# One-pass broadcasts of stacked high and low parts, and row halves of the array in turn, in a two-block sequence model

## The chip, the cores and the metric

The kernel runs on one core of one Trainium2 chip. The metric is device time in microseconds (us); the number that counts is the median of several runs. The engines have their own in-order instruction queues: TensorE (PE; its weight loads stand apart as PEld), VectorE (DVE), ScalarE (ACT), GpSimd (POOL) and SyncE (SP), which issues most of the DMAs.

## The reference

It computes one layer of a first block and two layers of a second one on a sequence of 512 positions with 1024 features. In the first block attention over a band of chunks stands beside an S5 state-space mixer, then come memory attention and a table of 16384 experts, of which each position picks some. A layer of the second block has three branches, of which two use decays along the sequence (SSD and a gated delta rule, GDN), then a feed-forward part. What the change touches:

```python
def _rmsnorm(x, g):
    xf = x.astype(jnp.float32)
    y = xf * lax.rsqrt(jnp.mean(xf * xf, axis=-1, keepdims=True) + EPS)
    return (y * g.astype(jnp.float32)).astype(x.dtype)
...
    bu_r = jnp.einsum('blgc,gpc->blgp', uf, bbr)
    bu_i = jnp.einsum('blgc,gpc->blgp', uf, bbi)
...
    y = (jnp.einsum('blgp,gcp->blgc', xr, c_re.astype(jnp.float32))
         - jnp.einsum('blgp,gcp->blgc', xi, c_im.astype(jnp.float32))
         + d_skip.astype(jnp.float32) * uf)
...
    L = jnp.exp(jnp.where(tril, A_cum[..., :, None] - A_cum[..., None, :], -jnp.inf))
...
    decay = jnp.exp(jnp.where(incl, g[..., :, None] - g[..., None, :], -jnp.inf))
```

Norms need one number per position, and decays one number per position and head, for all features at once.

## The kernel before

Activations lie with features on the 128 partitions and positions along the free axis, 512 (`T`) at a time. Large products are made of three one-pass products (`mm3`, lines 162 to 164): a value is split into a high part `H` and a low part `L` (`split`: ScalarE rounds to `H`, line 140; VectorE subtracts, line 141), and high times high, high times low and low times high are summed in PSUM. Small products are left in fp32, which the array does in more than one pass; the trace has two records for each.

Work is written as Python generators that run in turn, and the tile framework sets the order in which each engine issues; TensorE then works through its list in that order. PSUM has five buffers named `s`, two `g` and one `o`.

Four places matter here.

- A number per position on one column, `r` (128 positions by 4 blocks), comes from `rsqrt` on VectorE (its last line is 134). `rowbc` (line 179) makes of it a row that stands on all 128 partitions: for each block of 128 positions it takes the column, repeated 128 times, as weights, and the identity as the moving operand (line 183), four fp32 products. It serves every norm: 38 calls on 512 columns, five on 256 (in `memory_kv`). In `pair` of `mixers` four transpositions (816), a copy (818) and two products with the selecting matrix `sel` of 4 rows (821) do the same for two heads at once, four times.
- `Layer.rows` (line 1435) puts the cumulated decay of head `j` on all partitions: the transposed decays are kept as `cumT`, a high and a low tensor of 24 rows, and two one-pass products of 24 rows (line 1440) with a column of a 24 by 24 identity sum them. It is called 16 times by `ssd` (two calls at once) and 8 times by `gdn_prep_pair` in each of the two layers, that is 48 times.
- `S5.matrices` makes, for each of four blocks of groups, the taps `kt` (lines 607, 608): 16 products of 64 rows with 16 output rows, first all of the lower 64 partitions (`gh` 0), then all of the upper. They go by a POOL DMA to `kd` and back as `toep`.
- `S5.run` makes the outputs of a block: for each of its eight groups one product with `toep` (128 rows, line 661) and two of 64 rows with `car` and `cai` (662, 663), one group after the other.

Of the kernel before, what the change touches and what calls it, by code (L numbers as in the profile page):

```python
# [11 lines left out]
F32 = mybir.dt.float32  # L12
F32R = mybir.dt.float32r
I32 = mybir.dt.int32
U32 = mybir.dt.uint32
AF = mybir.ActivationFunctionType
OP = mybir.AluOpType
# [4 lines left out]
P = 128  # L22
T = 512
# [3 lines left out]
def f32(ap):  # L27
    return ap.bitcast(F32)
# [21 lines left out]
class Builder:  # L50
# [65 lines left out]
        self.tri = tri  # L116


    def rsqrt(self, out, x, scale, eps):

        nc, shape = self.nc, list(x.shape)
        v = self.small(shape)
        nc.vector.tensor_scalar(v, x, float(scale), float(eps), op0=OP.mult, op1=OP.add)
        sh = self.small(shape, I32)
        nc.vector.tensor_scalar(sh, v.bitcast(I32), 1, None, op0=OP.logical_shift_right)
        y = self.small(shape)
        nc.vector.tensor_scalar(y.bitcast(I32), sh, -1, 0x5F3759DF, op0=OP.mult, op1=OP.add)
        for i in range(3):
            a = self.small(shape)
            nc.vector.tensor_tensor(a, y, y, op=OP.mult)  # L130
            b = self.small(shape)
            nc.vector.scalar_tensor_tensor(b, a, -0.5, v, op0=OP.mult, op1=OP.mult)
            y2 = out if i == 2 else self.small(shape)
            nc.vector.scalar_tensor_tensor(y2, b, 1.5, y, op0=OP.add, op1=OP.mult)
            y = y2
# [43 lines left out]

    def rowbc(self, ps, col, n=T):  # L180

        for tb in range(n // P):
            self.nc.tensor.matmul(ps[:, tb * P:(tb + 1) * P],  # L183
                                  col[:, tb:tb + 1].to_broadcast([P, P]), self.ident,
                                  start=True, stop=True)

    def sumsq(self, srcs, n=T, w2=None):
        nc = self.nc
# [298 lines left out]
class S5:  # L487
# [57 lines left out]
    def matrices(self, q):  # L545
# [5 lines left out]
        m = t([P, 4, 4, 16], "s5m", 1)  # L551
# [45 lines left out]
                                B.ident[:16, :16].unsqueeze(1).to_broadcast([16, 8, 16]), op=OP.mult)  # L597
        kd = B.t([16, 8, 15, 16], F32, "kd", 2, B.dr)

        for gh in range(2):  # L600
            kt = t([16, 4, 15, 16], "kt")
            nc.vector.memset(kt[:, :, 0:7], 0.0)
            lo = 64 * gh
            ps = B.pss()
            for g in range(4):
                o = ps[:16, g * P:(g + 1) * P]
                nc.tensor.matmul(o, bbr[lo:lo + 64, g], car[lo:lo + 64, g, 0:8], start=True, stop=False)
                nc.tensor.matmul(o, bbi[lo:lo + 64, g], cai[lo:lo + 64, g, 0:8], start=False, stop=True)
            nc.scalar.copy(kt[:, :, 7:15], ps[:16].rearrange("p (g k c) -> p g k c", g=4, k=8))
            yield  # L610
            nc.vector.tensor_tensor(kt[:, :, 7], kt[:, :, 7], dd[:, gh::2], op=OP.add)
            nc.gpsimd.dma_start(kd[:, gh::2], kt)
# [5 lines left out]
    def run(self, u, mats, outer):  # L618
# [34 lines left out]
            v.tensor_tensor(out[:, :, 1:64], x[:, :, 0:63], y[:, :, 0:63], op=op)  # L653
        yg = t([P, 8, 64], "yg", 1)
        yield
        for gh in range(2):
            lo = 64 * gh
            ps = B.pss()
            for g in range(4):
                o = ps[:, 64 * g:64 * g + 64]  # L660
                nc.tensor.matmul(o, toep[:, 2 * g + gh], U[:, 2 * g + gh], start=True, stop=False)
                nc.tensor.matmul(o, car[lo:lo + 64, g, 1:9], xr[lo:lo + 64, g], start=False, stop=False)
                nc.tensor.matmul(o, cai[lo:lo + 64, g, 1:9], xi[lo:lo + 64, g], start=False, stop=True)
            nc.scalar.activation(yg[:, gh::2], ps[:, :256].rearrange("p (g j) -> p g j", g=4), AF.Gelu)
        yd = B.t([8, 16, 8, 64], F32, "yd", 2, B.dr)
        for s in range(8):
            nc.sync.dma_start(yd[:, :, s].rearrange("g c j -> c g j"), yg[16 * s:16 * s + 16])
# [62 lines left out]
def mixers(B, vec, memory, new_h):  # L730
# [3 lines left out]
    with tc.tile_pool(name="mixers", bufs=1) as pool:  # L734
# [2 lines left out]
        nc.vector.memset(hm[0:64, 0:1], 1.0)  # L737
        nc.vector.memset(hm[64:128, 1:2], 1.0)

        sel = B.t([4, 2, P], F32, "sel", 1, pool)  # L740
        nc.vector.memset(sel, 1.0)
        for base, sign in ((0, 1), (63, -1)):
            nc.gpsimd.affine_select(out=sel, in_=sel, pattern=[[P * sign, 2], [sign, P]], compare_op=OP.is_ge,
                                    fill=0.0, base=base, channel_multiplier=-64 * sign)
        xq = [B.t([P, T], F32, "qk", 8, pool) for _ in range(8)]
        for k in range(8):
            nc.sync.dma_start(xq[k], B.d["xT"][k])
# [47 lines left out]
        def pair(j):  # L795
# [18 lines left out]
            rt = B.pss()  # L814
            for tb in range(4):
                nc.tensor.transpose(rt[:4, tb * P:(tb + 1) * P], r[:, 4 * tb:4 * tb + 4], B.ident)
            rT = B.w2()[:4]
            nc.scalar.copy(rT, rt[:4])
            for i in range(2):
                ps = B.pss()  # L820
                nc.tensor.matmul(ps, sel[:, i], rT, start=True, stop=True)
# [408 lines left out]
class Second:  # L1230
# [5 lines left out]
    def setup(self, pool):  # L1236
# [20 lines left out]
            aff(c3, c3, [[s, P // s], [0, s]], OP.is_gt, 0.0, s, -1)  # L1257
        v.tensor_tensor(self.cross, self.cross, self.blk, op=OP.subtract)
        v.tensor_tensor(self.cross, self.cross, self.low, op=OP.mult)
        self.eye = B.t([24, 24], F32R, "eye", 1, pool)  # L1260
        v.tensor_copy(self.eye, B.ident[:24, :24])
        yield

        self.rot = B.t([P, P], F32R, "rot", 1, pool)
# [22 lines left out]
class Layer:  # L1287
# [73 lines left out]
    def decays(self, xs, rs):  # L1361
# [57 lines left out]
        pt = B.pss()  # L1419
        for tb in range(4):  # L1420
            nc.tensor.transpose(pt[:24, tb * P:(tb + 1) * P], self.cum[:, tb], B.ident)
        self.cumT = [B.t([24, T], F32R, "cumT" + k, 1, pool) for k in "HL"]
        B.split(pt[:24], *self.cumT)

        self.etot, self.eleft = t([P, 4, 24], "etot"), t([P, 4, 24], "eleft")
        nc.scalar.activation(self.etot, tot, AF.Exp)
# [7 lines left out]
    def rows(self, j):  # L1434

        B = self.B
        ps = B.pss()
        one = self.S.eye[:, j:j + 1].to_broadcast([24, P])
        for k, x in enumerate(self.cumT):
            B.nc.tensor.matmul(ps, one, x, start=k == 0, stop=k == 1)  # L1440
        return ps


# [561 lines left out]
```

## Time and profile before

| what | value |
|---|---|
| median of 3 runs | 4712.33 us (4710.74 to 4717.49) |
| the profiled execution | 4713.34 us |
| its span, first to last instruction | 4711.3 us |
| PE busy | 4638.6 us (98%), 22296 instructions |
| DVE busy | 2838.5 us (60%) |
| ACT busy | 1905.1 us (40%) |
| chain that ended last | PE 88%, DVE 8%, DMA 1%, ACT 1% |
| mean granted TensorE clock | 0.987 |

A busy share says how long some instruction of the engine was under way. Records of products overlap, so what a product costs in a stream is the distance from its start to the start of the next. The chain is followed back from the last instruction, at each step to what released it. The granted clock is given as a share of 2.4 GHz; it is 1.0 or 0.5 at any moment.

### The profile page before, as it was taken

To read this page: it belongs to the slowest core of one execution; us is meant where nothing else is said; L and a number is where in the kernel's file an instruction comes from. 1 tells how busy PE (TensorE), PEld (TensorE's weight loads), DVE (VectorE), ACT (ScalarE), POOL (GpSimd) and SP (SyncE) were. 2 spreads that over 40 slices of the span, in tenths; PEclk is the share of its full clock that TensorE was granted. 3 is DMA by queue.
4 is the path that set the end of the run, shared out by engine and by line. 5 is a ranking of instruction groups with operands and counts; after the bars stand their busy time and mean duration, and the time that the engine had idled before them with its cause. 6 is when DMAs were issued, how large, how long until landed. Compare 5 with 4: busy or idle time off the path is not lost.

```text
span 4711.3 us, 59345 instructions
## 1 busy us (share of the span) xinstructions
PE 4638.6 (98%) x22296; PEld 3718.0 (79%) x22296; DVE 2838.5 (60%) x5744; ACT 1905.1 (40%) x3652; POOL 29.0 (1%) x59
## 2 busy tenths in 40 slices
PE   8989999999999999999999999999999999999998
PEld 6777788888888888887787678888877876888887
DVE  8655799665545555556776545544478765545434
ACT  3343458763222222323553433333355535333322
POOL 0000000000000000000000000000000000000000
PEclk9789999999999999999999999999999999999999
DMA  4232235564434443442254155423324532544332
GB/s 133 68 97 76 83 124 182 201 205 152 132 123 138 143 133 128 134 141 82 81 179 144 49 156 171 151 92 94 102 87 135 174 108 75 170 158 130 97 95 81
DMA packets 306047, 589.26 MB, mean 125 GB/s; under 512 B 60192, under 2 KB 147552, under 8 KB 303584
## 3 DMA queue, kind: packets, MB, share of 16 engines
q1 hardware_dynamic: 304480, 582.88, 38.6%
q0 software_dynamic: 1280, 2.59, 0.3%
q8 instruction: 175, 2.87, 0.3%
q14 instruction: 112, 0.92, 0.1%
HBM read 480.29 MB, written 105.09 MB: 124 GB/s over the span
## 4 chain that ended last, share of the span: by engine, by line
PE 88%; DVE 8%; DMA 1%; ACT 1%; issue 1%; SPq 0%; DVEq 0%; ACTq 0%
PE g L162 13%; PE g L163 13%; PE g L164 13%; PE o L162 6%; PE o L163 6%; PE o L164 6%; PE s L1191 5%; PE s L1192 5%; PE s L1190 5%; PE s L1137 3%; DVE wL L141 1%; PE s L249 1%; PE s L183 1%; PE s L1615 1%; DMA vr<-in_pv 1%
## 5 line engine op out<-in xcount | busy, mean ns | idle before, releaser
L140 ACT ACTIVATE wH<-wr 128x1024 fp32r<-128x1024 f32 (+2 forms) x599 | 602.3, 1006 | 1328.8 <-PE g L163 810.9
L141 DVE TENSOR_TENSOR wL<-wr,wH 128x1024 fp32r<-128x1024 f32 (+2 forms) x599 | 692.6, 1157 | 444.0 <-ACT wH L140 425.8
L162 PE MATMUL g<-xH,wH 128*128 128x512 f32 (+1 forms) x2328 | 921.3, 396 | 16.1 <-ACT wH L140 12.4
L164 PE MATMUL g<-xH,wL 128*128 128x512 f32 (+1 forms) x2328 | 917.0, 394 | 3.0 <-DVE wL L141 3.0
L163 PE MATMUL g<-xL,wH 128*128 128x512 f32 (+1 forms) x2328 | 919.1, 395 | 0.1
L162 PEld LDWEIGHTS g<-xH,wH 128*128 128x128 f32 x2328 | 443.0, 190 | 117.7 <-ACT wH L140 13.3
L164 PEld LDWEIGHTS g<-xH,wL 128*128 128x128 f32 x2328 | 442.7, 190 | 101.5 <-DVE wL L141 6.4
L163 PEld LDWEIGHTS g<-xL,wH 128*128 128x128 f32 x2328 | 443.1, 190 | 93.8 <-issue 2.6
L162 PE MATMUL o<-xH,wH 128*128 128x512 f32 x1032 | 411.9, 399 | 2.7 <-DVE wg L1318 1.8
L164 PE MATMUL o<-xH,wL 128*128 128x512 f32 x1032 | 411.2, 398 | 1.5 <-DVE wL L141 1.5
L163 PE MATMUL o<-xL,wH 128*128 128x512 f32 x1032 | 411.6, 399 | 0.0
L1191 PE MATMUL s<-WL,VH 128*128 128x512 f32 x1024 | 399.6, 391 | 2.3 <-DVE WL L141 2.3
L1190 PE MATMUL s<-WH,VH 128*128 128x512 f32 x1024 | 398.2, 391 | 0.2 <-ACT WH L140 0.2
L1192 PE MATMUL s<-WH,VL 128*128 128x512 f32 x1024 | 397.6, 389 | 0.0
L140 ACT ACTIVATE VH<-vr 128x1024 fp32r<-128x1024 f32 x128 | 132.4, 1056 | 543.4 <-PE s L1191 385.1
L1193 DVE TENSOR_TENSOR h<-h,s 128x512 f32<-128x512 f32 x256 | 174.0, 685 | 271.7 <-PE s L1192 271.7
L164 PE MATMUL g<-yH,wL 128*128 128x512 f32 x632 | 250.7, 397 | 3.0 <-DVE wL L141 3.0
L163 PE MATMUL g<-yL,wH 128*128 128x512 f32 x632 | 250.5, 396 | 0.3 <-DVE yL L230 0.3
L162 PE MATMUL g<-yH,wH 128*128 128x512 f32 x632 | 250.5, 397 | 0.0
L141 DVE TENSOR_TENSOR VL<-vr,VH 128x1024 fp32r<-128x1024 f32 x128 | 154.1, 1223 | 141.8 <-ACT VH L140 141.6
L162 PEld LDWEIGHTS o<-xH,wH 128*128 128x128 f32 x1032 | 194.4, 188 | 49.0 <-issue 5.2
L164 PEld LDWEIGHTS o<-xH,wL 128*128 128x128 f32 x1032 | 194.4, 188 | 45.9 <-DVE wL L141 2.4
(636 smaller groups left out, 7139.5 us busy)
## 6 DMA issues: line engine op xcount, KB each, us to landing
wr<-in_w_in SPq DMA_DIRECT2D x166, 512.0 KB, 3.6
wr<-in_pu SPq DMA_DIRECT2D x128, 512.0 KB, 4.2
vr<-in_pv SPq DMA_DIRECT2D x128, 512.0 KB, 3.8
gd<-G SPq DMA_DIRECT2D x16, 2048.0 KB, 6.6
gt<-gd SPq DMA_DIRECT2D x64, 512.0 KB, 5.4
wr<-in_w_o SPq DMA_DIRECT2D x64, 512.0 KB, 3.6
wr<-in_w_up SPq DMA_DIRECT2D x64, 512.0 KB, 3.5
wr<-in_w_dn SPq DMA_DIRECT2D x64, 512.0 KB, 3.6
```

The lines of the kernel that those rows point to most:

```text
L140: nc.scalar.activation(H, src, AF.Copy)
L141: nc.vector.tensor_tensor(L, src, f32(H), op=OP.subtract)
L162: nc.tensor.matmul(ps, wH[:, k], xH, start=s, stop=False)
L163: nc.tensor.matmul(ps, wH[:, k], xL, start=False, stop=False)
L164: nc.tensor.matmul(ps, wL[:, k], xH, start=False, stop=e)
L183: self.nc.tensor.matmul(ps[:, tb * P:(tb + 1) * P], col[:, tb:tb + 1].to_broadcast([P, P]), self.ident, start=True, stop=True)
L249: self.nc.tensor.transpose(ps[:, tb * P:(tb + 1) * P], src[:, tb * P:(tb + 1) * P], self.ident)
L1137: nc.tensor.matmul(ps[:, j * P:(j + 1) * P], o2[:, k], og[:, j], start=True, stop=True)
L1190: nc.tensor.matmul(ps, VH[:, n], WH, start=k == 0, stop=False)
L1191: nc.tensor.matmul(ps, VH[:, n], WL, start=False, stop=False)
L1192: nc.tensor.matmul(ps, VL[:, n], WH, start=False, stop=k == 3)
L1193: nc.vector.tensor_tensor(h[n], h[n], ps, op=OP.add)
```

## The change

- `consts` makes `eye` for all: 128 by 24, with a one in row `c` and in row `32 + c` of column `c`; and two tensors `parts` of 128 by 128, zeroed once.
- `rowbc` first transposes the columns (4 by 128), and `split2` writes the high part of it to rows 0 to 3 and the low part to rows 32 to 35 of one of the two `parts`, which are used in turn. Then it makes one one-pass product of 128 rows per block, with a column of `eye`, repeated, as weights: high and low are summed within the product.
- `rows` does the same with one `cumT` of 128 rows, which is zeroed in every layer, and one product in place of two. `pair` does the same with `sel` in 128 rows and an `rT` that GpSimd zeroes each time.
- `S5.matrices` and `S5.run` hold two PSUM tiles, one for each half `gh`, and put products of the lower and the upper 64 rows in turn; in `S5.run` the eight products with `toep` come first.

```diff
+        self.eye = self.t([P, 24], F32R, "eye")
+        nc.vector.tensor_tensor(self.eye, ident[:, :24], ident[:, 32:56], op=OP.add)
+
+        self.parts = [self.t([P, P], F32R, f"rT{i}") for i in range(2)]
+        for x in self.parts:
+            nc.vector.memset(f32(x), 0.0)
...
     def rowbc(self, ps, col, n=T):
 
-        for tb in range(n // P):
-            self.nc.tensor.matmul(ps[:, tb * P:(tb + 1) * P],
-                                  col[:, tb:tb + 1].to_broadcast([P, P]), self.ident,
-                                  start=True, stop=True)
+        nb = n // P
+        self.nc.tensor.transpose(ps[:nb, :P], col, self.ident)
+        x = self.parts[0]
+        self.parts.reverse()
+        self.split2(ps[:nb, :P], x)
+        for tb in range(nb):
+            self.nc.tensor.matmul(ps[:, tb * P:(tb + 1) * P], self.eye[:, tb:tb + 1].to_broadcast([P, P]), x, start=True, stop=True)
+
+    def split2(self, src, x):
+
+        n = src.shape[0]
+        self.split(src, x[:n], x[32:32 + n])
...
+        pss = [B.pss() for _ in range(2)]
+        for g in range(4):
+            for k, (a, b) in enumerate(((bbr, car), (bbi, cai))):
+                for gh in range(2):
+                    lo = 64 * gh
+                    nc.tensor.matmul(pss[gh][:16, g * P:(g + 1) * P], a[lo:lo + 64, g], b[lo:lo + 64, g, 0:8],
+                                     start=k == 0, stop=k == 1)
         for gh in range(2):
             kt = t([16, 4, 15, 16], "kt")
             nc.vector.memset(kt[:, :, 0:7], 0.0)
-            lo = 64 * gh
-            ps = B.pss()
-            for g in range(4):
-                o = ps[:16, g * P:(g + 1) * P]
-                nc.tensor.matmul(o, bbr[lo:lo + 64, g], car[lo:lo + 64, g, 0:8], start=True, stop=False)
-                nc.tensor.matmul(o, bbi[lo:lo + 64, g], cai[lo:lo + 64, g, 0:8], start=False, stop=True)
-            nc.scalar.copy(kt[:, :, 7:15], ps[:16].rearrange("p (g k c) -> p g k c", g=4, k=8))
+            nc.scalar.copy(kt[:, :, 7:15], pss[gh][:16].rearrange("p (g k c) -> p g k c", g=4, k=8))
...
+        pss = [B.pss() for _ in range(2)]
         for gh in range(2):
-            lo = 64 * gh
-            ps = B.pss()
             for g in range(4):
-                o = ps[:, 64 * g:64 * g + 64]
-                nc.tensor.matmul(o, toep[:, 2 * g + gh], U[:, 2 * g + gh], start=True, stop=False)
-                nc.tensor.matmul(o, car[lo:lo + 64, g, 1:9], xr[lo:lo + 64, g], start=False, stop=False)
-                nc.tensor.matmul(o, cai[lo:lo + 64, g, 1:9], xi[lo:lo + 64, g], start=False, stop=True)
-            nc.scalar.activation(yg[:, gh::2], ps[:, :256].rearrange("p (g j) -> p g j", g=4), AF.Gelu)
+                nc.tensor.matmul(pss[gh][:, 64 * g:64 * g + 64], toep[:, 2 * g + gh], U[:, 2 * g + gh],
+                                 start=g == 0, stop=False, skip_group_check=True)
+        for g in range(4):
+            for m, x in ((car, xr), (cai, xi)):
+                for gh in range(2):
+                    lo = 64 * gh
+                    nc.tensor.matmul(pss[gh][:, 64 * g:64 * g + 64], m[lo:lo + 64, g, 1:9], x[lo:lo + 64, g],
+                                     start=False, stop=m is cai and g == 3, skip_group_check=True)
+        for gh in range(2):
+            nc.scalar.activation(yg[:, gh::2], pss[gh][:, :256].rearrange("p (g j) -> p g j", g=4), AF.Gelu)
...
-        sel = B.t([4, 2, P], F32, "sel", 1, pool)
-        nc.vector.memset(sel, 1.0)
...
+        sel = B.t([P, 2, P], F32R, "sel", 1, pool)
+        nc.vector.tensor_copy(sel.rearrange("p a (b d) -> p (a b) d", d=64),
+                              f32(B.eye)[:, 0:4].unsqueeze(2).to_broadcast([P, 4, 64]))
...
-            rT = B.w2()[:4]
-            nc.scalar.copy(rT, rt[:4])
+            rT = B.w2(F32R)
+            nc.gpsimd.memset(f32(rT), 0.0)
+            B.split2(rt[:4], rT)
...
-        self.cumT = [B.t([24, T], F32R, "cumT" + k, 1, pool) for k in "HL"]
-        B.split(pt[:24], *self.cumT)
+        self.cumT = B.t([P, T], F32R, "cumT", 1, pool)
+        v.memset(f32(self.cumT), 0.0)
+        B.split2(pt[:24], self.cumT)
...
-        one = self.S.eye[:, j:j + 1].to_broadcast([24, P])
-        for k, x in enumerate(self.cumT):
-            B.nc.tensor.matmul(ps, one, x, start=k == 0, stop=k == 1)
+        B.nc.tensor.matmul(ps, B.eye[:, j:j + 1].to_broadcast([P, P]), self.cumT, start=True, stop=True)
```

The lines below are the issue order of an engine: line, operation, output<-inputs, shape. First TensorE at the outputs of the second S5 block, before; `g` are the large products of attention around it, `hm` those of a head's square sum.

```order
L164 MATMUL g_1950<-xH_126,wL_1947 128x512
L177 MATMUL g_2153<-ones_63,acc_2130 128x1 x2
L661 MATMUL s_1900<-U_1727,toep_1635 128x64
L662 MATMUL s_1900<-x_1822,car_1245 128x64
L661 MATMUL s_1914<-U_1727,toep_1635 128x64
L662 MATMUL s_1914<-x_1822,car_1245 128x64
L809 MATMUL s_1939<-hm_74,w_555_1870 128x2 x4
L809 MATMUL s_1939<-hm_74,w_576_1977 128x2 x4
L663 MATMUL s_1900<-x_1823,cai_1246 128x64
L661 MATMUL s_1900<-U_1727,toep_1635 128x64
```

The same place of the changed kernel, where `s_1913` and `s_1914` are the PSUM tiles of the two halves:

```order
L172 MATMUL g_1963<-xH_130,wL_1960 128x512
L185 MATMUL g_2168<-ones_63,acc_2145 128x1 x2
L678 MATMUL s_1913<-U_1738,toep_1646 128x64 x4
L678 MATMUL s_1914<-U_1738,toep_1646 128x64 x4
L684 MATMUL s_1913<-x_1835,car_1254 128x64
L684 MATMUL s_1914<-x_1835,car_1254 128x64
L684 MATMUL s_1913<-x_1836,cai_1255 128x64
L684 MATMUL s_1914<-x_1836,cai_1255 128x64
```

Products of 128 and of 64 rows no longer alternate; those of 64 rows alternate between the halves, and the square sums of the heads have moved behind the block.

Next, TensorE at the norms of `q` and `k` in `gdn_prep_pair` (third pair of the first layer), before:

```order
L163 MATMUL g_20427<-xL_18283,wH_20423 128x512
L164 MATMUL g_20427<-xH_18282,wL_20424 128x512
L183 MATMUL s_20409<-ident_65,sm_4350_20341 128x128 x4
L183 MATMUL s_20415<-ident_65,sm_4350_20341 128x128 x4
L162 MATMUL g_20427<-xH_18288,wH_20423 128x512
```

And in the changed kernel (`rT_5` and `rT_6` are the two `parts`):

```order
L172 MATMUL g_20480<-xH_18337,wL_20477 128x512
L191 MATMUL s_20456<-ident_65,sm_4351_20388 4x128
L191 MATMUL s_20465<-ident_65,sm_4351_20388 4x128
L170 MATMUL g_20480<-xH_18343,wH_20476 128x512
L171 MATMUL g_20480<-xL_18344,wH_20476 128x512
L172 MATMUL g_20480<-xH_18343,wL_20477 128x512
L196 MATMUL s_20456<-rT_6_72,eye_69 128x128 x4
L196 MATMUL s_20465<-rT_5_71,eye_69 128x128 x4
L170 MATMUL g_20480<-xH_18349,wH_20476 128x512
```

Three large products now stand between the transpositions and the products that use them. VectorE's list there, in the changed kernel, from the last step of the root on:

```order
L142 SCALAR_TENSOR_TENSOR sm_4351_20388<-sm_4362_20409,sm_4360_20405 128x8
L149 TENSOR_TENSOR rT_6_72<-s_20456,rT_6_72 4x128
L149 TENSOR_TENSOR rT_5_71<-s_20465,rT_5_71 4x128
L1704 SCALAR_TENSOR_TENSOR q_20320<-q_20320,s_20456 128x512
L1704 SCALAR_TENSOR_TENSOR k_20321<-k_20321,s_20465 128x512
L149 TENSOR_TENSOR wL_20593<-wr_20590,wH_20592 128x1024
```

The two subtractions have come in between the root and the scaling of `q`; the rest stands as before.

## Rows read from the trace of the kernel before

**Rows 1.** Windows: stretch, its us, engines' busy us, then granted clock, DMA.

```profile
60.00:360.00 300.00, 282.05 (x1594) 218.76 (x1595) 202.14 (x669) 120.13 (x282) 21.17 (x40) 0.85 0.32 88
...
161.00:176.00 15.00, 14.67 (x65) 12.84 (x65) 9.05 (x43) 2.90 (x5) 0.00 (x0) 0.59 0.05 17
...
360.00:4690.00 4330.00, 4303.37 (x20475) 3456.90 (x20474) 2576.05 (x4815) 1759.48 (x3331) 6.31 (x11) 1.00 0.40 127
```

**Rows 2.** TensorE's waits: line, who ended them: us in total, times, longest.

```profile
PE g L162 <- ACT wH L140: 12.4, 1, 12.4
PE g L164 <- DVE wL L141: 6.0, 9, 1.3
PE s L183 <- DVE sm L134: 4.9, 2, 2.4
...
PE s L821 <- ACT w L818: 3.8, 1, 3.8
```

**Rows 3.** Timeline of TensorE, start and duration in us: `rows` in `ssd`, then `gdn_prep_pair`.

```profile
2250.97 0.49 PE L1440 MATMUL s<-cumTH,eye 24*128 24x512 f32 x1
...
2252.08 0.49 PE L163 MATMUL g<-xL,wH 128*128 128x512 f32 x1
...
2355.01 0.40 PE L163 MATMUL o<-xL,wH 128*128 128x512 f32 x1
2355.24 0.40 PE L164 MATMUL o<-xH,wL 128*128 128x512 f32 x1
2355.57 0.49 PE L1440 MATMUL s<-cumTH,eye 24*128 24x512 f32 x1
...
2356.22 0.50 PE L162 MATMUL g<-xH,wH 128*128 128x512 f32 x1
2356.56 0.39 PE L163 MATMUL g<-xL,wH 128*128 128x512 f32 x1
```

**Rows 4.** Timeline of TensorE: a `rowbc` in a stream; four transpositions in a stream.

```profile
27.38 0.60 PE L249 MATMUL s<-ident,w 128*128 128x128 f32 x4
27.73 0.47 PE L163 MATMUL g<-xL,wH 128*128 128x512 f32 x1
...
2188.75 1.05 PE L183 MATMUL s<-ident,sm 128*128 128x128 f32 x8
2189.56 0.48 PE L164 MATMUL g<-yH,wL 128*128 128x512 f32 x1
2189.88 0.39 PE L162 MATMUL g<-yH,wH 128*128 128x512 f32 x1
```

**Rows 5.** Groups by form: count, busy us, mean ns, idle before: ScalarE, VectorE.

```profile
L1815 ACT COPY vn<-s 128x128 f32<-128x128 f32 x64 | 17.0, 266 | 33.4 <-PE s L1813 30.0 <-PE s L1811 3.4
...
L1780 DVE TENSOR_TENSOR ti<-ti,s 64x128 f32<-64x128 f32 x16 | 4.4, 272 | 0.0
```

**Rows 6.** The page's groups, same columns: VectorE's half of the weight splits.

```profile
L141 DVE TENSOR_TENSOR wL<-wr,wH 128x1024 fp32r<-128x1024 f32 (+2 forms) x599 | 692.6, 1157 | 444.0 <-ACT wH L140 425.8
```

**Rows 7.** Groups by form, TensorE: the products with `sel`.

```profile
L821 PE MATMUL s<-w,sel 4*128 4x512 f32 x16 | 9.7, 734 | 3.8 <-ACT w L818 3.8
```

**Rows 8.** Timeline of TensorE in `mla`: 64-row products of two heads in turn.

```profile
2627.83 1.13 PE L1608 MATMUL s<-kpe,qpe 64*128 64x512 f32 x4
2628.89 0.38 PE L1604 MATMUL s<-kn,qn 128*128 128x128 f32 x1
```

**Rows 9.** Timeline of TensorE: groups of S5 outputs, second block, then fourth block.

```profile
167.33 0.69 PE L661 MATMUL s<-U,toep 128*128 128x64 f32 x2
...
168.99 0.69 PE L661 MATMUL s<-U,toep 128*128 128x64 f32 x2
...
285.80 0.43 PE L661 MATMUL s<-U,toep 128*128 128x64 f32 x2
...
286.75 0.43 PE L661 MATMUL s<-U,toep 128*128 128x64 f32 x2
```

**Rows 10.** Timeline of VectorE: idle before, and what ended it, in brackets.

```profile
181.76 0.21 DVE L611 TENSOR_TENSOR kt<-kt,dq 16x64 f32<-16x64 f32 x1 [11.69 <-ACT kt L609]
```

More of the change, by code (lines that the diff above doesn't have):

```diff
@@ L738, in mixers @@
         nc.vector.memset(hm[64:128, 1:2], 1.0)
-        sel = B.t([4, 2, P], F32, "sel", 1, pool)
-        nc.vector.memset(sel, 1.0)
-        for base, sign in ((0, 1), (63, -1)):
-            nc.gpsimd.affine_select(out=sel, in_=sel, pattern=[[P * sign, 2], [sign, P]], compare_op=OP.is_ge,
-                                    fill=0.0, base=base, channel_multiplier=-64 * sign)
+        sel = B.t([P, 2, P], F32R, "sel", 1, pool)
+        nc.vector.tensor_copy(sel.rearrange("p a (b d) -> p (a b) d", d=64),
+                              f32(B.eye)[:, 0:4].unsqueeze(2).to_broadcast([P, 4, 64]))
         xq = [B.t([P, T], F32, "qk", 8, pool) for _ in range(8)]
@@ L1259, in setup @@
         v.tensor_tensor(self.cross, self.cross, self.low, op=OP.mult)
-        self.eye = B.t([24, 24], F32R, "eye", 1, pool)
-        v.tensor_copy(self.eye, B.ident[:24, :24])
         yield
```

## The prediction

> **What bounds the kernel now.** I read the windows first. From 360 to 4690 us TensorE is busy 4303 of 4330 us at a full granted clock; from 60 to 360 us, the mixers' stage, 282 of 300 us at a mean clock of 0.85, while VectorE has 202 and ScalarE 120 us there [rows 1]. At 0.85 some 90 of these 300 us ran at the lower level, 1.2 GHz (300 x 0.15 / 0.5). The table of waits then says who ends TensorE's few idle times: outside the start (12.4 us), no line waits more than 6.0 us in all [rows 2]. So TensorE's issue order is the kernel's path, and a microsecond of array time removed comes back as time, as long as what takes its place isn't a wait. What must be read is not the busy time of a product, whose records overlap, but the distance from one start to the next.
>
> **1. The products of `rows`.** In a stream of 128-row products one starts every 0.23 us (2355.01 to 2355.24). The pair of 24-row products costs more than two of these: 0.33 us to its first start, 0.66 to the next line's start, 0.34 to the one after [rows 3]. From 2355.24 to 2356.56 that is 1.32 us; less two ordinary distances (0.46) the pair costs 0.86. Afterwards it is one product of 128 rows, of the form that its neighbours have: 0.23. So 0.63 saved, for the 16 calls of `gdn_prep_pair` 10.1 us. In `ssd` two calls stand together: 2250.97 to 2252.08 is 1.11 us for four products [rows 3]; two products take 0.46, and 0.05 remains, I assume, because the neighbours there fill 64 columns. 0.60 x 16 pairs = 9.6 us. Together **19.7 us**, all of it in streams where TensorE never waits: nothing is late next, since `cumT`, which they read, was made long before.
>
> **2. `rowbc`.** Its four fp32 products are eight records: 0.81 us to the next start, and the one after comes at 0.32 in place of 0.23: 0.90 in all, 0.10 per record [rows 4]. What comes instead: one transposition and four one-pass products of 128 columns. The trace has no such product. Its price lies between a quarter of a 512-column one (0.06) and a 128-column transposition, four of which take 0.35 us to the next start, with the same 0.09 behind them: 0.11 each [rows 4]. I take 0.11, since that row has the same weight load of 128 columns. So 5 x 0.11 = 0.55, saved 0.35; at 0.06 it would be 0.55. With 38 calls on 512 columns: 13.3 us (up to 21).
>
> The Trainium skill ("TensorE: Matmul & The Clock Gate", section "Back-to-back issue gap") gives about 81 ns for a 128-column product in a stream of load and product; by that the four would take 0.32, and the sum would have 4.6 us more of gain. The transpositions of this trace, at 0.11, don't agree, and I go by them.
>
> Against it stands a new wait. The chain is now transposition, ScalarE, VectorE, product: 0.27 us for a ScalarE copy of 128x128 out of PSUM, 0.27 for a VectorE subtraction of 64x128 [rows 5], as much, I take, for the transposition to its last column, and some 0.05 at each hand-over: 0.95 us. TensorE issues in order, so all behind the product waits too. The order of the changed kernel shows what stands between: at 16 of the 38 places five rows or more (over 1.1 us: covered), at 18 three or four (four products are 0.92 us, just the bare chain), at 4 two or fewer. For the 18 I put 0.3 us, a part of one large split ahead in a queue (1.16 us in the mean on VectorE [rows 6]): 5.4 us lost. At the 4 the whole chain is bare, 0.95 + 0.55 against 0.90 now: 0.5 each, 2 us. These are places where TensorE waits for the root already, up to 2.4 us [rows 2]. Net **6 us** gained, with bounds from 14 (0.06 a product, the same waits) to a loss (rivals B and E). The five calls on 256 columns in `memory_kv` run two and two through the two buffers, four of them at the lower clock; I put 1 us gained there. The zeroing of `parts`, `eye` and the new `sel` move VectorE at the start by under half a microsecond, and what waits there waits for ScalarE first [rows 2]: 0.2 us.
>
> **3. The mixers' stage.** (a) `sel`: 16 records of fp32 with 4 rows take 9.7 us [rows 7]; eight one-pass products take 8 x 0.23 = 1.8 us, 2.3 with a quarter at the lower clock. 7 us. The subtraction of 4x512 and GpSimd's zeroing are new on its chain. The memset of `rT` stands on the POOL queue ahead of the DMAs to `kd` and `toep`, so that these wait where its buffer comes free late; the first waits in the table name neither [rows 2], and I put nothing. If a zeroing is late, TensorE waits at `sel`, as it already does once for 3.8 us [rows 2]. (b) `kt`: 128 records with 64 rows at 0.11 are 14.1 us, 17 with a block at the lower clock. Do halves run side by side? Yes: four records of 64 rows and 512 columns, two in either half, take 1.06 us to the next line's start [rows 8], where four times 512 columns at 0.10 per 128 [rows 4] would be 1.6 one after the other, and two 0.8; the rest is the change of form at either end. So half: 8 us. (c) the output products: `toep` (128 rows), `car`, `cai` (64 rows) in turn take 0.95 us per group at the full clock and 1.66 at the lower one [rows 9]. Blocks have 8 groups; the second runs at a mean clock of 0.59 [rows 1]. Before: 24 x 0.95 + 8 x 1.66 = 36 us. After, a block is 16 `toep` records and 16 side-by-side pairs at 0.11 each, and two changes of form at 0.1: 3.7, at the lower clock 7.2. 3 x 3.7 + 7.2 = 18; 18 us saved.
>
> Together 33 us of array time. In the second block it is plainly the path: VectorE sits idle 11.7 us until `kt` is copied, which waits for these very products [rows 10]. Elsewhere the softmax and the scan will now be late more often; VectorE is busy two thirds of the stage. I take 85%: **28 us**, between 12 and 50 (the latter if the lower clock goes too).
>
> **Sum.** 19.7 + 6 + 1 + 28 - 0.2 = 54.5 us. The profiled execution took 4713.3 us, 2.0 more than its span and 1.0 more than the median of the runs, 4712.3. From the median: 4712.3 - 54.5 = **4658 us**.
>
> **Rivals.** *B, the hop eats `rowbc`*: the 18 tight places and half of the 16 others wait 1 us each, the length of one split. Then 26 us are lost in place of 5.4: 4679. For it: 34 new waits in front of a queue that issues in order; against: the order on VectorE has the subtraction right behind the root, ahead of the next split. *C, the clock stays up*: the clock falls inside the 64-row products (0.95 becomes 1.66 [rows 9]); with these halved it may not fall, and if half of the 90 us at 1.2 GHz go, about 22 us more come back: 4636. *D, TensorE is no longer the bound in the mixers' stage*, or the halves don't overlap at 64 columns so that the change doesn't do what it says: of 28 us a third remains: 4677. *E, slower*: at each of the 34 places in streams both queues have a large split ahead, 1.2 us each [rows 6], nothing covers them, and as VectorE waits in its turn, the next weights are split late by as much again: 34 x 4.6 = 156 us lost, 60 gained: 4808. It decides from (54.5 + 5.4) / 34 = 1.8 us per place. Against it: at `rowbc` now, whose input has the same queue ahead, waits sum to 4.9 us [rows 2]. *F, the clock falls at `rowbc`*: fewer fp32 columns, a transposition in their place. If each of the 34 places lost 2 us of clock: 4720. Against it: the long stretch, which has transpositions throughout, holds 1.00 [rows 1].
>
> The Trainium skill (same page, section "Part 4: PE-mode transpose") says that transpose mode doesn't count as busy for the clock in the same way; that is the rule which speaks for F. The stretch from 360 to 4690 us doesn't bear it out.
>
> **How the numbers follow.** Forecast 0.58, B 0.14, C 0.11, D 0.11, E 0.03, F 0.03. 0.2% (9 us) is about what a measurement tells from no change. Faster: forecast, C and all but the far tails of B and D, 0.90; same 0.05, from those tails and F; slower 0.05, E and half of F. The range takes in B, D and C's own spread but not E and F: 4627 to 4690.
>
> **What would show it.** `rows`: one product, 0.23 to the next start in `gdn_prep_pair`. `rowbc`: 0.55 in all; a wait named "VectorE `rT`" on TensorE, 5 to 10 us in sum. A block's output products in under 4 us at the full clock, starts of two halves a few ns apart. From 60 to 360 us, the stage some 28 us shorter; from 360 on, 26. Wrong if the wait for `rT` is over 20 us, or the stage is shorter by under 12.

## The result, and the profile after

The changed kernel took 4662.41 us (median of four runs, 4661.44 to 4666.07), the kernel before, on the same chip, 4714.91 us. The ratio is 0.9888, with an interval of 0.9876 to 0.9901: 52.5 us less, between 46.7 and 58.5. The forecast was 54.5 us less and 4658 us. The sum was good; its terms were not, as the single parts below show.

The profiled execution is the longest of the four (4666.07, span 4664.4). So I compare it with the one before by stretches, from one product of weights to the same product in the other kernel (their starts are the bounds of the windows below). The planner, the part of the tile framework that sets each engine's order, can write the stage of the mixers in another order when the kernel changes, so only such marks bound the same work. Here are the windows, in the columns of [rows 1]: first the kernel before, then the changed one.

```profile
12.45:385.02 372.57, 352.51 (x1898) 275.10 (x1899) 256.87 (x898) 144.34 (x319) 21.17 (x40) 0.88 0.33 94
385.02:2069.95 1684.93, 1679.44 (x7858) 1371.60 (x7856) 1049.39 (x2080) 707.51 (x1292) 3.56 (x9) 1.00 0.43 140
2069.95:4689.92 2619.97, 2598.83 (x12511) 2064.94 (x12510) 1515.64 (x2723) 1044.30 (x2029) 2.75 (x2) 1.00 0.38 119
```

```profile
12.78:351.87 339.09, 307.59 (x1876) 247.05 (x1877) 261.06 (x910) 145.95 (x327) 23.32 (x44) 0.91 0.35 103
351.87:2042.38 1690.51, 1679.76 (x7839) 1368.08 (x7838) 1049.82 (x2084) 708.63 (x1298) 3.02 (x9) 1.00 0.42 139
2042.38:4642.81 2600.43, 2571.43 (x12379) 2047.93 (x12377) 1522.32 (x2753) 1047.09 (x2058) 2.53 (x2) 1.00 0.38 120
```

The first stretch, the start and the mixers, lost 33.5 us; the second gained 5.6; the third, with `rows` and most of `rowbc`, lost 19.5. In the first, TensorE's idle time rose from 20.1 to 31.5 us (length less busy), and the time at 1.2 GHz, summed from the clock records, fell from 88.7 to 58.0 us, which is worth at most half of the 30.7, 15.4. What remains, 33.5 + 11.4 - 15.4 = 29.5 us, is array time. So three things moved where the forecast had one. In the third stretch idle time rose from 21.1 to 29.0 us and busy time fell by 27.4.

The rows of the changed kernel that answer to [rows 4], [rows 3] and [rows 9] follow, all from its timeline of TensorE. First, a `rowbc` in a stream: the transposition, six products, then the four one-pass products.

```profile
2161.01 0.39 PE L171 MATMUL g<-yL,wH 128*128 128x512 f32 x1
2161.24 0.27 PE L191 MATMUL s<-ident,sm 128*4 128x128 f32 x1
2161.27 0.48 PE L172 MATMUL g<-yH,wL 128*128 128x512 f32 x1
2161.58 0.39 PE L170 MATMUL g<-yH,wH 128*128 128x512 f32 x1
...
2162.98 0.64 PE L196 MATMUL s<-rT,eye 128*128 128x128 f32 x4
2163.46 0.44 PE L170 MATMUL g<-yH,wH 128*128 128x512 f32 x1
2163.74 0.39 PE L171 MATMUL g<-yL,wH 128*128 128x512 f32 x1
...
2342.49 0.40 PE L1459 MATMUL s<-cumT,eye 128*128 128x512 f32 x1
2342.73 0.40 PE L170 MATMUL g<-xH,wH 128*128 128x512 f32 x1
...
255.36 1.89 PE L678 MATMUL s<-U,toep 128*128 128x64 f32 x16
257.19 0.44 PE L684 MATMUL s<-x,car 64*128 64x64 f32 x4
257.46 0.39 PE L684 MATMUL s<-x,cai 64*128 64x64 f32 x4
257.68 0.39 PE L684 MATMUL s<-x,car 64*128 64x64 f32 x4
...
259.12 0.44 PE L265 MATMUL g<-ident,wm 128*128 128x128 f32 x2
```

The transposition costs 0.03 to the next start and 0.31 in place of 0.23 to the one after, 0.11; the four products 0.48 here and 0.41 at the median place, with 0.05 behind them. Together 0.57, against 0.90 before: the forecast had 0.55. `rows` costs 0.24, as forecast. A block of S5 outputs takes 3.76 us, from 255.36 to 259.12 (forecast 3.7 at the full clock), and four records of 64 rows take 0.22 us, so two halves run at once. The Trainium skill ("TensorE: Matmul & The Clock Gate", section "Part 3: Packing small matmuls — row/col tiling") says that products on different row groups run together; these rows agree, at 0.11 us for a pair.

The waits of TensorE in the changed kernel that answer to [rows 2]; the columns are the same.

```profile
PE g L170 <- ACT wH L148: 12.8, 1, 12.8
PE g L170 <- DVE wg L1338: 9.8, 3, 3.9
PE g L172 <- DVE wL L149: 6.8, 9, 2.0
...
PE o L170 <- ACT w L704: 4.8, 1, 4.8
...
PE s L843 <- DVE w L149: 4.0, 1, 4.0
...
PE s L196 <- DVE rT L149: 3.4, 6, 0.8
...
PE g L196 <- DVE rT L149: 0.8, 1, 0.8
```

The new wait, for `rT`, is 4.2 us in seven places, less than the 5.4 + 2 that I had put. But others grew: for `wg` in `ssd` 9.8 (2.9 before), for `w` of the mixers' end 4.8 (0.9 before).

### The profile page after: what moved, and what is told of

Its sections match the earlier page's. It is cut to its first block, busy times and chain, and to the rows that moved or that the text cites. A ratio compares the mean times of both kernels' runs of the same rounds, so it can differ in the third digit from the quotient of the medians.

```text
span 4664.4 us, 59083 instructions
## 1 busy us (share of the span) xinstructions
PE 4566.1 (98%) x22121; PEld 3668.7 (79%) x22121; DVE 2850.5 (61%) x5795; ACT 1911.1 (41%) x3695; POOL 29.6 (1%) x61
## 4 chain that ended last, share of the span: by engine, by line
PE 83%; DVE 7%; DMA 3%; ACT 1%; issue 1%; SPq 0%; DVEq 0%; ACTq 0%
PE g L171 13%; PE g L170 13%; PE g L172 13%; PE o L170 6%; PE o L171 6%; PE o L172 6%; PE s L1213 5%; PE s L1214 5%; PE s L1212 4%; PE s L1159 3%; DVE wL L149 2%; PE s L265 1%; DMA vr<-in_pv 1%; DMA ga<-ad 1%; PE s L1634 1%
```

## The experiments

Each was timed in up to eleven runs against the kernel before on its own chip; differences in us are the ratio less one, times 4714. For each profile I give the first stretch and the third, bounded by the same products as above: length, idle time of TensorE, and time at 1.2 GHz, all in us. "Full" is the length less the idle time and less half of the time at 1.2 GHz: what is left if the clock had stood at 2.4 GHz. It can be off where idle time and low clock coincide.

| kernel | ratio, interval | first: length, idle, 1.2 GHz, full | third: length, idle, 1.2 GHz, full |
|---|---|---|---|
| before | 1 | 372.6, 20.1, 88.7, 308.1 | 2620.0, 21.1, 20.5, 2588.6 |
| changed | 0.9888, 0.9876 to 0.9901 | 339.1, 31.5, 58.0, 278.6 | 2600.4, 29.0, 23.9, 2559.5 |
| rows_alone | 0.9962, 0.9949 to 0.9976 | 375.0, 19.9, 95.6, 307.3 | 2603.0, 26.4, 20.5, 2566.4 |
| rowbc_alone | 1.0009, 1.0000 to 1.0018 | 381.7, 25.0, 102.4, 305.5 | 2609.3, 20.8, 6.8, 2585.1 |
| s5_alone | 0.9910, 0.9897 to 0.9924 | 333.3, 26.1, 30.7, 291.9 | 2622.5, 21.3, 27.3, 2587.6 |
| sel_alone | 1.0005, 0.9996 to 1.0014 | 368.1, 24.9, 81.9, 302.3 | 2622.3, 21.5, 17.1, 2592.3 |
| half_by_half | 0.9911, 0.9897 to 0.9924 | 351.5, 26.6, 68.3, 290.7 | 2598.1, 29.4, 20.5, 2558.5 |
| rows_s5 | 0.9882, 0.9866 to 0.9897 | 331.8, 23.8, 34.1, 290.9 | 2603.1, 27.8, 17.1, 2566.8 |
| late_rowbc | 0.9881, 0.9866 to 0.9896 | 331.4, 22.9, 34.1, 291.4 | 2600.9, 30.5, 23.9, 2558.5 |
| ten_old | 0.9880, 0.9864 to 0.9895 | 337.6, 26.6, 54.6, 283.7 | 2599.6, 29.8, 23.9, 2557.8 |
| ten_old_sel | 0.9874, 0.9859 to 0.9889 | 336.0, 22.8, 41.0, 292.7 | 2596.1, 30.1, 13.7, 2559.2 |
| no_hop | 0.9889, 0.9874 to 0.9904 | 336.0, 30.9, 51.2, 279.5 | 2599.1, 29.3, 20.5, 2559.6 |
| free_hop | 0.9913, 0.9899 to 0.9926 | 346.3, 35.5, 58.0, 281.8 | 2595.5, 28.0, 17.1, 2559.0 |
| no_split | 0.9867, 0.9852 to 0.9882 | 331.4, 27.3, 41.0, 283.7 | 2595.0, 27.6, 17.1, 2558.9 |

How well a stretch repeats in one profile is seen where a kernel has the same code in it as before: the third one of s5_alone and sel_alone is 2.5 and 2.3 us longer, the first one of rows_alone 2.4, with 6.8 us more at 1.2 GHz. The first stretch of s5_alone, rows_s5, late_rowbc and ten_old_sel, which has the same products of TensorE in nearly the same order in all four, takes 331.4 to 336.0 us. So a difference of under 5 us in one stretch shows nothing by itself.

**One part at a time.** Four kernels put one part of the change into the kernel before.

```diff
-        for k, x in enumerate(self.cumT):
-            B.nc.tensor.matmul(ps, one, x, start=k == 0, stop=k == 1)
+        B.nc.tensor.matmul(ps, B.eye[:, j:j + 1].to_broadcast([P, P]), self.cumT, start=True, stop=True)
```

> The kernel before with only the products of rows changed: 48 calls of one 128-row product on the stacked cumT in place of two 24-row ones. Forecast (array time comes back as time): 16 x 0.63 + 16 x 0.60 = 19.7 us faster, 17 to 21 allowed. Rival (the weights' split is late next and takes half of it): 10 us. Rival (form changes cost nothing, only the second product goes): 48 x 0.23 = 11 us. In the trace one product in gdn_prep_pair costs 0.23 us to the next start.

17.9 us faster (11 to 24); in the third stretch 17.0 us, 22.2 of it by "full", of which 5.3 went to new idle time. The forecast holds, with a part handed back to waits.

```diff
-            self.nc.tensor.matmul(ps[:, tb * P:(tb + 1) * P],
-                                  col[:, tb:tb + 1].to_broadcast([P, P]), self.ident,
-                                  start=True, stop=True)
+        self.nc.tensor.transpose(ps[:nb, :P], col, self.ident)
...
+        self.split2(ps[:nb, :P], x)
+        for tb in range(nb):
+            self.nc.tensor.matmul(ps[:, tb * P:(tb + 1) * P], self.eye[:, tb:tb + 1].to_broadcast([P, P]), x, start=True, stop=True)
```

> The kernel before with only rowbc changed, 43 calls. Forecast: 7 us faster (13.3 of array time, 5.4 and 2 lost to the hop, 1 in memory_kv); the trace of the changed kernel already shows few waits for rT, so up to 12 us. Rival B (the hop eats it): 13 us slower. Rival F (the transpositions cost clock): 30 us slower, with stretches at 1.2 GHz behind the places of rowbc.

4.2 us slower (0 to 8.5). Neither the forecast nor the sizes of rivals B and F. The third stretch, where 28 of the 43 calls stand, is 10.6 us shorter, though up to 6.8 of that are the clock's (20.5 to 6.8 us at 1.2 GHz); the one between is 4.2 longer. The first is 9.1 longer, with its array time 2.6 less: 4.9 us more are idle time, and 13.7 us more run at 1.2 GHz, half of which rows_alone shows as well. Its window, in the columns of [rows 1], and then the largest of its new waits, 0.9 before:

```profile
12.83:394.49 381.66, 356.69 (x1884) 277.26 (x1885) 259.97 (x906) 146.57 (x327) 21.19 (x40) 0.87 0.32 92
```

```profile
PE o L167 <- ACT w L695: 5.3, 1, 5.3
```

That wait is for the mixers' end, not for a broadcast row; in s5_alone, with the old `rowbc`, it is 4.4.

```diff
-                nc.tensor.matmul(o, toep[:, 2 * g + gh], U[:, 2 * g + gh], start=True, stop=False)
-                nc.tensor.matmul(o, car[lo:lo + 64, g, 1:9], xr[lo:lo + 64, g], start=False, stop=False)
-                nc.tensor.matmul(o, cai[lo:lo + 64, g, 1:9], xi[lo:lo + 64, g], start=False, stop=True)
+        for g in range(4):
+            for m, x in ((car, xr), (cai, xi)):
+                for gh in range(2):
...
```

> The kernel before with only the S5 products changed: kt and the outputs alternate between the row halves, toep products first. Forecast: 26 us of array time, 85% of it back: 22 us faster, between 12 and 40. Rival C (the clock stays up in the second block too): 35 us or more, and the 37.5 us stretch at 1.2 GHz behind 163.6 us gone or under half. Rival D (TensorE then waits for the softmax and the scan): under 12 us, with TensorE's waits from 60 to 360 us up by over 10 us.

42.4 us faster (36 to 49): rival C. The time at 1.2 GHz in the first stretch falls from 88.7 to 30.7 us, and the piece of 37.5 us that begins in the second block of outputs is gone; rows_alone, rowbc_alone and sel_alone, which keep the old S5 products, all have a piece of 37.5 us there. These are the windows from 160 to 180 us, first of rowbc_alone, then of s5_alone (the granted clock is the third number from the right):

```profile
160.00:180.00 20.00, 19.66 (x88) 16.94 (x87) 12.35 (x54) 4.93 (x8) 0.00 (x0) 0.64 0.10 30
```

```profile
160.00:180.00 20.00, 14.81 (x92) 9.43 (x92) 18.51 (x102) 10.55 (x38) 2.94 (x6) 0.83 0.32 70
```

In the first, TensorE is busy 19.66 of 20 us, with the old products of the second block in it, and the mean clock is 0.64. In the second, it is busy less, and the clock is 0.83. The price is 6.0 us more idle time.

The clock records of the kernel before show where the clock falls: once inside each of its four blocks of outputs, at 119.2, 163.6, 228.4 and 289.9 us, and in the first, third and fourth TensorE doesn't wait at all. These rows are from the fourth; the distance of two `car` records to the next start goes from 0.27 to 0.48 us:

```profile
289.01 0.43 PE L662 MATMUL s<-x,car 64*128 64x64 f32 x2
289.28 0.38 PE L663 MATMUL s<-x,cai 64*128 64x64 f32 x2
289.60 0.45 PE L661 MATMUL s<-U,toep 128*128 128x64 f32 x2
289.98 0.69 PE L662 MATMUL s<-x,car 64*128 64x64 f32 x2
290.46 0.63 PE L663 MATMUL s<-x,cai 64*128 64x64 f32 x2
```

In s5_alone and in the changed kernel the clock falls in none of the four blocks. The first stretch takes 331 to 352 us in all ten kernels with the new S5 products and 368 to 382 in the four with the old, so the gain doesn't hang on one order of the stage.

```diff
-            rT = B.w2()[:4]
-            nc.scalar.copy(rT, rt[:4])
+            rT = B.w2(F32R)
+            nc.gpsimd.memset(f32(rT), 0.0)
+            B.split2(rt[:4], rT)
```

> The kernel before with only the products of pair with sel changed: 8 one-pass products of 128 rows in place of 16 records of 4-row fp32. Forecast: 7 us of array time, 6 us faster, between 3 and 9. Rival (the chain with its zeroing and subtraction is later than the products are shorter): 0 to 4 us slower, TensorE's wait at the products over 6 us in the trace.

2.4 us slower, from 1.9 faster to 6.6 slower: no change. The profiled execution, one of the shorter of its eleven runs, has the 5.9 us of array time less, and 4.8 more idle, half of it at one S5 output product:

```profile
PE s L827 <- DVE w L143: 4.0, 1, 4.0
...
PE s L669 <- DVE x L660: 2.5, 1, 2.5
```

These are rows of its table of waits from 60 to 390 us. The wait at the products themselves stays what it was, 4.0 against 3.8; the 2.5 us for the scan's `x` stood at 0.3 in the kernel before. The rival had the wait at the wrong place, but the outcome is nearer to it.

The four differences add up to -53.7 us, the whole change measured -52.5. So the parts explain the whole, but not in the shares that I had forecast.

**Is it the halves?** In the changed kernel the loops over `gh` and `g` were exchanged for the 64-row products alone:

```diff
-        for g in range(4):
-            for m, x in ((car, xr), (cai, xi)):
-                for gh in range(2):
+        for gh in range(2):
+            for g in range(4):
+                for m, x in ((car, xr), (cai, xi)):
```

> The changed kernel with its S5 products of 64 rows issued one half after the other (all of the lower half, then all of the upper), toep products still first: only the alternation is undone. Theory (halves run side by side): 64 output products and 64 kt products no longer overlap, 128 x 0.11 = 14 us more than the changed kernel's 4662, so 4676, between 4670 and 4682. Rival (the gain is from the order, toep first, and the halves don't overlap): 4662. Rival (the alternation is what keeps the clock up): over 4685, with a stretch at 1.2 GHz of more than 20 us between 140 and 190 us.

4674.21 us, 11 us more by the ratios. "Full" of the first stretch rises by 12.1 us; counted from starts, `kt` costs 6.7 and the outputs 6.7 us more. The theory holds: the halves overlap, and that is worth 12 to 14 us. It is not the whole of the S5 gain. With `toep` first and no alternation the outputs take 22.3 us, against 39.0 in the kernel before and 15.6 in the changed one, so most of their gain comes with the order and the clock; no run has the alternation without `toep` first. The timeline of its fourth block says something of the clock besides:

```profile
264.30 1.89 PE L678 MATMUL s<-U,toep 128*128 128x64 f32 x16
266.13 0.43 PE L684 MATMUL s<-x,car 64*128 64x64 f32 x2
266.40 0.38 PE L684 MATMUL s<-x,cai 64*128 64x64 f32 x2
266.62 0.38 PE L684 MATMUL s<-x,car 64*128 64x64 f32 x2
...
268.52 0.63 PE L684 MATMUL s<-x,car 64*128 64x64 f32 x2
268.95 0.63 PE L684 MATMUL s<-x,cai 64*128 64x64 f32 x2
```

TensorE never waits here. Two records take 0.22 us at 266.40 and 0.43 at 268.52: the clock fell to 1.2 GHz while 64-row products ran one half after the other. In the changed kernel, whose fourth block stands above, they keep 0.22 for four records to the end. At the second block, whose outputs run from 153.8 to 160.0, a piece of 20.5 us at 1.2 GHz begins at 159.2; but the changed kernel has as much from 157.5 to 188.2 us, in three pieces, behind waits. In the whole stretch the time at 1.2 GHz rises by 10.3 us, from 58.0 to 68.3, of the 30.7 that the change had taken away. So the third rival of that run has its mechanism in the fourth block, but not its size: the alternation alone doesn't keep the clock up.

**What does `rowbc` cost?** Three kernels keep its instructions on TensorE and change what these wait for; their broadcast rows are left out.

```diff
-        x = self.parts[0]
-        self.parts.reverse()
-        self.split2(ps[:nb, :P], x)
+        self.split2(ps[:nb, :P], self.parts[0])
+        x = self.parts[1]
```

> The changed kernel with all its transpositions, splits and one-pass products of rowbc, but the products read the tile of parts that stays zero, so that none waits for its split (the broadcast rows are left out). Theory (what rowbc gains in streams is lost to the hop at the few bare places and to what follows them): 10 to 16 us faster than the changed kernel, 4648, with TensorE's waits before 500 us down by 4 us or more. Rival (the added work on ScalarE and VectorE is what costs, the hop is covered): 4662, as the changed kernel.

4664.52 us, as the changed kernel. But the edit did not take the hop away: the products write the PSUM tile that the split reads, so they still wait for it, and the trace still names `rT` at the products. The run tells nothing; free_hop was made for it.

```diff
-        self.split2(ps[:nb, :P], self.parts[0])
+        self.split2(self.ident[:nb, :P], self.parts[0])
```

> The changed kernel with rowbc's split still run on ScalarE and VectorE, but from the identity in SBUF, and the products reading the tile that stays zero: nothing on TensorE waits for the split any more, neither through its output nor through the PSUM tile that it reads (the broadcast rows are left out). Theory (the hop costs what rowbc should have gained): 10 us faster than the changed kernel, 4652. Rival (the hop is covered and costs under 4 us, as the waits for rT of the trace say): 4659 to 4664.

```diff
-        self.split2(ps[:nb, :P], self.parts[0])
```

> As the kernel before this, with the 43 splits left out altogether (86 instructions fewer on ScalarE and VectorE; the broadcast rows are left out). Theory (the added work in the two queues delays the splits of weights): 5 to 10 us faster than with the free hop, 4645 to 4655. Rival (the queues have room): within 3 us of it.

free_hop took 4670.97 us, 12 more than the changed kernel by the ratios, although no wait for a split stands in its trace: the theory of the hop falls, and its rival was too low as well. no_split took 4649.57: 10 less than the changed kernel, with intervals that just overlap, and 22 less than free_hop, beyond both intervals. In the third stretch the two are alike (2595.5 and 2595.0), so in the streams the queues have room. Both are about 5 us under the changed kernel there, but 6.8 us less at 1.2 GHz are up to 3.4 of these, idle time is 1.0 to 1.4 and "full" 0.5: the hop in the streams costs little. Most of the difference of the two stands in the first stretch: 346.3 against 331.4.

That first stretch doesn't settle by which way. Without the splits, or without their dependence, the planner writes another order: TensorE's instructions of free_hop differ from those of the changed kernel from 20.1 us on, and a wait of 3.6 us for the S5 rotation's `sm` stands at the start:

```profile
PE g L170 <- ACT wH L148: 13.1, 1, 13.1
PE g L170 <- DVE sm L499: 3.6, 1, 3.6
```

These are rows of its table of waits from 12 to 70 us; no_split has no wait over 0.2 us up to 60 us but the first. How much of rowbc's cost in the mixers' stage is the two new instructions in the queues, and how much is the order that the planner makes of them, stays open.

**Better versions.** From the parts: the new `rowbc` only where it gains, the old products with `sel`.

```diff
+        self.calls = getattr(self, "calls", 0) + 1
+        if self.calls in (1, 2, 3, 4, 5, 6, 7, 8, 13, 43):
+            for tb in range(n // P):
+                self.nc.tensor.matmul(ps[:, tb * P:(tb + 1) * P],
+                                      col[:, tb:tb + 1].to_broadcast([P, P]), self.ident,
+                                      start=True, stop=True)
+            return
```

> The changed kernel with the old rowbc (four fp32 products) at ten of the 43 calls: the first, the seven before and in the mixers' stage, the one ahead of the product with mk, and the last, where a row of the changed kernel shows a bare chain. Theory (these ten lose what the other 33 gain): 10 us faster than the changed kernel, 4652, between 4646 and 4657. Rival (the loss of rowbc alone is spread over waits for weights and has no place): 4662 or more, as ten calls lose their 0.35 us gain.

> As the kernel with the old rowbc at ten calls, and with the old products with sel as well. Theory (sel alone gave nothing, because its zeroing and split make TensorE wait): 2 us faster than that kernel, 4650. Rival (with the S5 products short, sel's 7 us of array time count): 4 to 7 us slower than that kernel, 4658.

4658.91 and 4656.10 us, 3.8 and 6.6 less than the changed kernel by the ratios, with intervals that overlap. The first lies between its theory (10) and its rival (0), so the ten calls are part of the loss at most; the second is 2.8 under the first, as its theory had (2).

The other two leave `sel` and `rowbc` as before, late_rowbc with the new `rowbc` in the calls 15 to 42 (the edit is the one above, with `self.calls < 15 or self.calls == 43`).

> The kernel before with the two parts that gained alone, rows and the S5 products; rowbc and sel as before. Theory (the parts add up): 17.9 + 42.4 = 60 us faster than before, 4655. Rival (the new rowbc's 33 calls in the kernel with the old one at ten calls are worth the 10 us that the trace shows from 2070 us on): 10 us slower than that kernel, 4666.

> As the kernel with rows and S5 alone, with the new rowbc at the 28 calls from 2070 us on, all in streams, the last call left out. Theory (in streams rowbc gains what the starts show, 0.33 us a call): 9 us faster than with rows and S5 alone, 4646, and the stretch behind 2070 us shorter by 9. Rival (the waits for weights give it back): the same as rows and S5 alone, 4655.

4657.11 and 4656.22 us. The two parts alone give -55.6 us, 4.7 less than their sum, within the intervals: these runs show no gain that `rowbc` and `sel` add. late_rowbc equals it, its rival. Its third stretch shows why: "full" falls by 8.2 us, near the gain that the starts promise, but idle time rises by 2.7 and 6.8 us more run at 1.2 GHz (3.4), so that 2.1 remain. The wait for `wg` alone, 6.9 us at two places in rows_s5, is 9.8 us at three in this row of late_rowbc's table of waits:

```profile
PE g L170 <- DVE wg L1346: 9.8, 3, 3.9
```

All three of these, ten_old_sel, rows_s5 and late_rowbc, are by the ratios 3 to 7 us under the changed kernel, with intervals that overlap with its own. That one of them is faster is not shown.

## Why the prediction was right, point by point

**The bound** was read rightly: TensorE's order is the path, and array time taken away comes back unless a wait replaces it. What I understated is the exception. Idle time of TensorE rose by 11.4 + 5.3 + 7.9 = 24.6 us over the three stretches; busy time fell by 72. I had put 5.4 + 2 for `rowbc` and 15% of the mixers' 33, 12 in all.

**`rows`**: forecast 19.7 us, 17.9 measured alone. One product costs 0.24 to the next start. In `ssd` two take 0.57 us where four took 1.11, and the product behind them 0.23 in place of 0.34, which my row left out: 0.65 saved in place of 0.60. The claim "nothing is late next" was wrong: 5.3 us of waits came, 4.0 of them at `wg` in `ssd` (6.9 us in rows_alone, 2.9 before).

**`rowbc`**: forecast 6 + 1 us faster, 4.2 slower alone. The price from starts was right (0.57 against 0.55), and the wait that carries its name was small, as forecast (4.2 us in place of 7.4). At a bare place the forecast's 0.95 + 0.55 against 0.90 is a loss of 0.6, not 0.5; the chain there takes 1.04 us from the transposition to the first product (at 4653.3 us, with nothing between). The step that failed is the choice to look for its cost at its own products. In rowbc_alone the cost came in the mixers' stage as waits at other products, such as the one for `w` of the mixers' end, and as time at 1.2 GHz, and in the second stretch as idle time; in the streams, once `rows` is shorter, as waits for `wg`. By which way the new `rowbc` brings these about stays open. Rival B named the right sign with the wrong mechanism.

**The mixers' stage**: forecast 28 us for `sel`, `kt` and the outputs together, 33.5 found in the profile, where `rowbc` in the same stage works against it. Alone, the S5 part gave 42.4 and `sel` nothing. By starts the array terms were right for what they counted: the outputs went from 39.0 to 15.6 us (forecast 36 to 18), `kt` from 18.3 to 10.4 (8 saved, as forecast), `sel` from 9.4 to 2.5 (7). But the clock was held fixed: I left a block at 1.2 GHz in the sum after the change, and put the case that it stays up, rival C, at 0.11. That was too low: the trace behind [rows 9] shows the clock falling inside the block of outputs without a wait in three of four blocks, and the change removes that pattern. A third of the time at 1.2 GHz went in the changed kernel (30.7 of 88.7 us), and two thirds in s5_alone (58.0).

**The sum** hit because the S5 part gave some 20 us more than its share of the forecast, while `rowbc`, `sel` and new waits took as much. The range was earned; the centre was luck.

**What would show it**: `rT` waits under the 5 to 10 us named; a block in 3.76 us, as named; the stage 33.5 us shorter in place of 28; from there on 14 in place of 26. Of the latter, 5.6 us are the second stretch, where only six `rowbc` calls were touched. It grew by 4.2 us in rowbc_alone as well. All but 0.3 us of the growth is idle time of TensorE: 9.1 to 13.5 us there in the eight profiles with the new `rowbc` in that stretch, free_hop and no_split among them, and 4.4 to 7.7 in the six with the old. So it goes with the new `rowbc`, and not with its splits alone. Of the waits that grew there, those for weights (`WL`, `wL`) are 2.8 us more, that for `mq` 1.4 and that for `rT` 0.6.

## What to carry to other kernels

When a kernel alternates products of half the array's rows, look at the granted clock inside them before pricing their removal: of the 39 us that s5_alone gained in its stage, up to 29 were the clock's. When array time is cut on a path that runs at 98% busy, find the next wait at every place where it is cut, since here a third of it came back as waits under other names. And time the parts alone, even when the sum is right; two of the four parts here showed no gain, and leaving them out cost nothing that these runs show.

## What the runs showed of the hardware

A fall of the clock to 1.2 GHz without any wait of TensorE: in the kernel before at 119.2, 228.4 and 289.9 us, inside blocks where products of 128 and of 64 rows alternate; in half_by_half at 268.4 us, in the middle of 64-row products on one half of the array, where the spacing of two records went from 0.22 to 0.43 us. With `toep` first and both halves in use, none of the changed kernel's four blocks of outputs shows it. A transposition with 4 columns of weights and 128 moving ones, in a stream of one-pass products, takes 0.11 us, the same as one of a 128-column one-pass product at the median (0.112).

The Trainium skill ("TensorE: Matmul & The Clock Gate", section "Back-to-back issue gap") gives about 81 ns for a 128-column product in a stream; the four here take 0.41 us at the median place, 0.10 each, and 0.46 with what they add to the next start, so the measurement decides.
